# Gate and up by quads of eight products, three of the eight with seven, in a hybrid encoder layer

## The chip, the cores and the metric

The kernel runs on one core of one Trainium2 chip. The metric is device time in microseconds (us) of one execution; lower is better. Before the change it is 1369.25 us, the median of three runs (1369.16 to 1369.85).

The engines by their names in the profile: PE is TensorE (matmuls; PEld its loads of the stationary operand), DVE is VectorE, ACT is ScalarE, POOL is GpSimd, and SP issues most DMAs. PSUM is the memory that matmuls write, eight banks of 512 float32 values per partition; SBUF is the large on-chip memory.

## The reference

One encoder layer on 256 tokens of width 2048, float32. The part that the change is about is the second half, a SwiGLU feed-forward network of width 5632:

```python
gt, up = jnp.split(rms_norm(x, g_ffn) @ w_gate_up, 2, axis=-1)
return x + (jax.nn.silu(gt) * up) @ w_down
```

Ahead of it stand a combined input projection, two attentions of eight heads each (latent attention and dilated window attention), sigmoid gates, and an output projection `w_o` that is added to the residual stream.

## The kernel before, in words

**Products in three parts.** A float32 product is made of three float32r matmuls. Each operand is split into `h`, its rounded copy, and `l`, the remainder. `mm3` (L383 to L386) issues h x h, then `ah` with the other operand's `l`, then `al` with its `h`, all added up in one PSUM bank. A *block product* here is `mm3` of 128 tokens by 128 features with 128 features by up to 512 columns.

**Groups and chunks.** All projections are `Group`s: a weight, 512 columns of it, a range of 128-row blocks k, and a function that reads the result out (`evac`). Each group has a PSUM tile of two banks, one per half of the tokens (`psm`, two tiles, tag "main"); transposes and attention use `side` tiles of two banks (`pss`, two of them). A group is cut into chunks of `CK` = 2 blocks. Per chunk there are three steps:

- `load(i)` (L694 to L703): one DMA of 512 KB on SP's queue into a tile of 4 KB per partition.
- `split(i)` (L705 to L712): ACT casts the chunk to `wh` (L710), DVE subtracts to get `wl` (L711).
- `products(i)` (L718 to L743): 2 blocks x 2 halves of the tokens x 3 matmuls = 12 matmuls.

The pool `wp` holds `AHEAD + 1` = 4 buffers of each of `w`, `wh` and `wl`. The pool `tp` holds 34 tiles of 4 KB per partition for activations (`t4`).

**What sets the order.** Each engine runs its instructions in the order of the program (L90 turns scheduling off); only semaphores between engines hold it. The loop at L781 to L815 is that order: at step i it issues the load of chunk i + 4, the split of chunk i + 3, the products of chunk i, then the read-out if the chunk ends its group, then at most one piece of a waiting job (a transpose, a stage of an attention). A job is `ready` some steps after it was made; if a product needs it sooner, it is finished on the spot (L789). A tile's buffer is given to a new tile when the old one's last reader is done.

**The feed-forward part.** The 22 blocks of 512 columns of `w_gate_up` are 11 of gate and 11 of up (L668 to L674), each a group of 16 blocks: 8 chunks. `evac_gate` (L592) applies silu on ACT, `evac_up` (L600) multiplies on DVE, and a job transposes the result into `hidT` (`transpose_in`, L196), whose own split is L171 on ACT and L176 on DVE. The columns are done in two halves, of six and five blocks; after each half come four groups of `w_down`, added to the residual `x1` by `evac_down` (L615). `evac_wo` (L568) makes `x1`, and its job transposes it with the gain `g_ffn` into `hT`, split likewise.

## Time and profile before

| | before |
|---|---|
| median of 3 runs | 1369.25 us |
| span of the profiled execution | 1367.5 us |
| TensorE busy | 1356.5 us (99%), 6342 matmuls |
| DVE busy | 758.1 us (55%), 774 instructions |
| ACT busy | 623.5 us (46%), 776 instructions |
| POOL busy | 32.3 us (2%) |
| DMA | 257.14 MB, 188 GB/s, queue of SP busy 59.8% |

The span is the time from the first to the last instruction of one profiled execution. "L711 DVE ... wl<-w,wh 128x1024" means that line 711 of the kernel ran on DVE, read the tiles w and wh, wrote wl, with 128 partitions by 1024 elements; then come how often, the busy time in us, the mean duration in ns, and the idle time of the engine just before with what ended it. A line of a timeline has its start in us, its duration in us, the engine, the line and the operation. Matmuls overlap in the pipeline, so the distance between two starts is their price, and not the duration shown.

The feed-forward part begins at 634.4 us of the span, with the first product of `hT`, and reaches to its end.

### The profile page before, as it was taken

The numbers are of one execution on the slowest core, as the hardware profiler recorded it, in microseconds if no ns is written. First come the engines' busy times: TensorE is split into PE (matmuls) and PEld (weight loads), VectorE is DVE, ScalarE is ACT, GpSimd is POOL, SyncE is SP. The second block draws the span as 40 slices with busy tenths as digits, with TensorE's granted clock in tenths as the row PEclk, the third lists the DMA queues.
The fourth block names the chain that finished last, engine by engine and source line by source line (L and its number), as shares of the span: only waits on it lengthen the run. The fifth ranks groups of instructions, "written<-read, shape, count | busy, mean of one in ns | idle before, by whom it ended". The sixth has DMA issues, their size and how long they took to land.

```text
span 1367.5 us, 16361 instructions
## 1 busy us (share of the span) xinstructions
PE 1356.5 (99%) x6342; PEld 1144.7 (84%) x6342; DVE 758.1 (55%) x774; ACT 623.5 (46%) x776; POOL 32.3 (2%) x41
## 2 busy tenths in 40 slices
PE   7999999999999999999999999999999999999998
PEld 6899999888888888888888888888888888888887
DVE  5566777677655556555445544554444544555443
ACT  6555655454444444445444444433344444444332
POOL 1011111000000000000000000000000000000000
PEclk9999999999999999999999999999999999999999
DMA  8555555555566666565665665555665665565663
GB/s 259 175 173 168 158 172 177 174 166 172 178 202 199 198 190 216 193 210 181 196 192 182 191 198 184 187 189 193 194 193 187 194 197 188 186 188 183 202 212 123
DMA packets 138205, 257.14 MB, mean 188 GB/s; under 512 B 9192, under 2 KB 28688, under 8 KB 138128
## 3 DMA queue, kind: packets, MB, share of 16 engines
q1 hardware_dynamic: 137760, 255.96, 59.8%
q8 instruction: 49, 0.80, 0.2%
q14 instruction: 28, 0.23, 0.0%
q10 hardware_dynamic: 144, 0.13, 0.0%
q0 software_dynamic: 224, 0.01, 0.0%
HBM read 253.97 MB, written 2.10 MB: 187 GB/s over the span
## 4 chain that ended last, share of the span: by engine, by line
PE 99%; DMA 1%; SPq 0%; DVE 0%; issue 0%; ACT 0%; DVEq 0%
PE g L384 31%; PE g L386 31%; PE g L385 31%; PE tr_hid L201 1%; DMA w<-in_w_in_dram 1%; PE tr_hT L201 0%; PE tr_mT L201 0%; PE tr_xT L201 0%; DMA xn<-in_x_dram 0%; PE mla3s L386 0%; PE mla2s L386 0%; PE mla0s L386 0%; PE mla1s L386 0%; PE mla2s L385 0%; PE mla2s L384 0%; PE mla1s L385 0%
## 5 line engine op out<-in xcount | busy, mean ns | idle before, releaser
L711 DVE TENSOR_TENSOR wl<-w,wh 128x1024 fp32r<-128x1024 f32 (+2 forms) x481 | 575.6, 1201 | 472.8 <-ACT wh L710 470.8
L710 ACT CAST wh<-w 128x1024 fp32r<-128x1024 f32 (+2 forms) x481 | 496.2, 1036 | 537.6 <-PE g L386 489.7
L384 PE MATMUL g<-wh,hTh 128*128 128x512 f32 x704 | 274.8, 390 | 0.0
L386 PE MATMUL g<-wh,hTl 128*128 128x512 f32 x704 | 274.0, 389 | 0.0
L385 PE MATMUL g<-wl,hTh 128*128 128x512 f32 x704 | 273.9, 389 | 0.0
L384 PE MATMUL g<-wh,xTh 128*128 128x512 f32 (+1 forms) x544 | 210.2, 386 | 1.9 <-ACT xTh L173 1.9
L386 PE MATMUL g<-wh,xTl 128*128 128x512 f32 (+1 forms) x544 | 207.2, 381 | 0.5 <-DVE xTl L178 0.5
L385 PE MATMUL g<-wl,xTh 128*128 128x512 f32 (+1 forms) x544 | 207.2, 381 | 0.0
L386 PEld LDWEIGHTS g<-wh,hTl 128*128 128x128 f32 x704 | 132.1, 188 | 27.6
L385 PEld LDWEIGHTS g<-wl,hTh 128*128 128x128 f32 x704 | 132.2, 188 | 27.1
L384 PEld LDWEIGHTS g<-wh,hTh 128*128 128x128 f32 x704 | 132.2, 188 | 27.1
L384 PEld LDWEIGHTS g<-wh,xTh 128*128 128x128 f32 x544 | 102.7, 189 | 17.2 <-ACT xTh L173 2.1
L386 PEld LDWEIGHTS g<-wh,xTl 128*128 128x128 f32 x544 | 102.4, 188 | 17.3 <-DVE xTl L178 1.0
L385 PEld LDWEIGHTS g<-wl,xTh 128*128 128x128 f32 x544 | 102.6, 189 | 15.3 <-DVE wl L711 0.4
L384 PE MATMUL g<-wh,hid0h 128*128 128x512 f32 x192 | 74.8, 390 | 0.0
L386 PE MATMUL g<-wh,hid0l 128*128 128x512 f32 x192 | 74.7, 389 | 0.0
L385 PE MATMUL g<-wl,hid0h 128*128 128x512 f32 x192 | 74.7, 389 | 0.0
L384 PE MATMUL g<-wh,hid1h 128*128 128x512 f32 x160 | 62.3, 390 | 0.0
L386 PE MATMUL g<-wh,hid1l 128*128 128x512 f32 x160 | 62.2, 389 | 0.0
L385 PE MATMUL g<-wl,hid1h 128*128 128x512 f32 x160 | 62.2, 389 | 0.0
L384 PE MATMUL g<-wh,mTh 128*128 128x512 f32 x128 | 50.2, 392 | 0.0
L386 PE MATMUL g<-wh,mTl 128*128 128x512 f32 x128 | 49.8, 389 | 0.0
(509 smaller groups left out, 1233.5 us busy)
## 6 DMA issues: line engine op xcount, KB each, us to landing
w<-in_w_gate_up_dram SPq DMA_DIRECT2D x176, 512.0 KB, 4.5
w<-in_w_down_dram SPq DMA_DIRECT2D x88, 512.0 KB, 4.3
w<-in_w_in_dram SPq DMA_DIRECT2D x79, 512.0 KB, 4.2
w<-in_w_in_dram SPq DMA_DIRECT2D x56, 448.0 KB, 3.6
w<-in_w_o_dram SPq DMA_DIRECT2D x32, 512.0 KB, 4.5
w<-in_w_o_mla_dram SPq DMA_DIRECT2D x16, 512.0 KB, 4.1
w<-in_w_o_dil_dram SPq DMA_DIRECT2D x16, 512.0 KB, 4.2
w<-in_w_ukv_dram SPq DMA_DIRECT2D x8, 512.0 KB, 4.3
```

The lines of the kernel that those rows point to most:

```text
L201: nc.tensor.transpose(ps[:, k, t * P:(t + 1) * P], src(t, k0 + k), ident)
L384: nc.tensor.matmul(ps, ah, bh, start=first, stop=False)
L385: nc.tensor.matmul(ps, ah, bl, start=False, stop=False)
L386: nc.tensor.matmul(ps, al, bh, start=False, stop=last)
L710: nc.scalar.copy(h, t)
L711: nc.vector.tensor_sub(l, t, f32(h))
```

## The change: what it does

**Quads.** A group of gate and up now has 1024 columns: 512 of gate and the 512 of up that belong to them (a *pair*; there are 11). Its 16 blocks of rows are 8 pairs of blocks. One *quad* is two row blocks (k0, k1) by gate and up, with both halves of the tokens: eight block products. Five quads (0, 1, 2, 4, 6) are *plain* and make these eight, 24 matmuls. Three (3, 5, 7, `FAST`) are *fast*: seven block products of sums and differences of the operands, 21 matmuls. The seven products have a PSUM bank each, kept over the whole pair; plain quads add to four places, three of them shared with fast products (banks of products 3, 2 and 4) and one of their own (0). All eight banks are taken from the start of the feed-forward part to the end (`hold_banks`). Transposes then use banks that are idle at that time.

**What a fast quad needs.** `split_fast` splits three raw quarters of the chunk (512 + 1024 columns: two casts on ACT, two subtractions on DVE), then forms four sums in place (four DVE additions of 512 columns). Then `split` splits the four sums (2048 columns). `splits` issues `split_fast` of chunk c + 1 ahead of `split` of chunk c. On the side of the activations, `job_h` transposes `x1` by pairs of blocks; for fast quads it forms four differences of 128 columns and splits seven pieces.

**The end of a pair.** `evac_pair` combines the banks: a copy on ACT, eight DVE operations of 512 columns, silu on ACT, two multiplications on DVE. Bank 0 is copied by ACT after quad 6.

**Chunks.** `CK` is 4, so a chunk is 1 MB (8 KB per partition), loaded by two DMAs of 512 KB. There are three raw buffers (`xp`), six of split weights (`wp`: h and l of three chunks), and 28 tiles of 4 KB instead of 34. Splits are issued two chunks ahead (`AHEAD` = 2), loads up to four ahead. For jobs and their readiness a step is still two row blocks, or one quad.

**Parts.** The 11 pairs are done in five parts of 3, 2, 2, 2 and 2, each followed by its four groups of `w_down`. These go two at a time, their chunks alternating, except for the last two of all.

The core of the diff:

```diff
-CK = 2
-AHEAD = 3
+CK = 4
+AHEAD = 2
+PARTS = ((0, 3), (3, 5), (5, 7), (7, 9), (9, 11))
+NPAIR = KD // 2
+FAST = (3, 5, 7)
...
-    wp = ctx.enter_context(tc.tile_pool(name="wp", bufs=AHEAD + 1))
-    tp = ctx.enter_context(tc.tile_pool(name="tp", bufs=34))
+    tp = ctx.enter_context(tc.tile_pool(name="tp", bufs=28))
+    xp = ctx.enter_context(tc.tile_pool(name="xp", bufs=3))
+    wp = ctx.enter_context(tc.tile_pool(name="wp", bufs=6))
...
+    def hold_banks():
+        for n in "AB":
+            held[n] = psm.tile([P, NT, 512], F32, name=f"m{n}", tag="main")
+        for n in "CD":
+            held[n] = side(f"s{n}").rearrange("p (t n) -> p t n", t=NT)
+        held["q"] = {m: held[n][:, i] for n, ms in (("A", (1, 6)), ("B", (7, 5)), ("C", (3, 2)), ("D", (4, 0)))
+                     for i, m in enumerate(ms)}
...
+        if i not in FAST:
+            hP[i] = t4([P, 2, 2, S], f"hP{i}", F32R)
+            split_evac(*((hP[i][:, 0, k], hP[i][:, 1, k], ps[:, k], g[k]) for k in range(2)))
+        else:
...
+            nc.vector.tensor_sub(v[:, 3], v[:, 7], v[:, 2])
+            nc.vector.tensor_sub(v[:, 4], v[:, 7], v[:, 0])
+            nc.vector.tensor_sub(v[:, 5], v[:, 0], v[:, 3])
+            nc.vector.tensor_sub(v[:, 6], v[:, 1], v[:, 5])
+            split_pair(h, l, v[:, :7])
...
+    def evac_pair(half, i, last):
+        def evac(part, step):
+            q = held["q"]
+            z, u = t4([P, NT, 512], f"z{half}_{i}"), t4([P, NT, 512], f"u{half}_{i}")
+            add, sub = nc.vector.tensor_add, nc.vector.tensor_sub
+            nc.scalar.copy(u[:, 0], q[1])
+            sub(z[:, 0], q[6], u[:, 0])
+            add(u[:, 1], q[7], z[:, 0])
+            add(z[:, 0], q[5], z[:, 0])
+            add(z[:, 1], q[5], u[:, 1])
+            add(z[:, 0], q[3], z[:, 0])
+            add(z[:, 1], z[:, 1], part)
+            add(u[:, 0], q[2], u[:, 0])
+            sub(u[:, 1], q[4], u[:, 1])
...
+    def load(c):
+        g, gi, ks, q = chunks[c]
+        t = xt[c] = xp.tile([P, 4, 512], F32, name=f"x{c}", tag="x")
+        if q:
+            for kk in range(2):
+                src = g.w[(2 * q.i + kk) * P:(2 * q.i + kk + 1) * P].rearrange("p (n f) -> p n f", n=2)
+                nc.sync.dma_start(t[:, 2 * kk:2 * kk + 2], src[:, :, g.c0:g.c0 + 512])
+            return
...
+    def split_fast(c):
+        x = xt[c]
+        rh, rl, r = (t4([P, 2, 512], f"{n}{c}", F32R) for n in ("rh", "rl", "r"))
+        split_pair(rh, rl, x[:, 2:4])
+        split_pair(r[:, 0], r[:, 1], x[:, 1])
+        add = nc.vector.tensor_add
+        add(x[:, 1], x[:, 0], x[:, 1])
+        add(x[:, 0], x[:, 0], x[:, 2])
+        add(x[:, 2], x[:, 1], x[:, 2])
+        add(x[:, 3], x[:, 2], x[:, 3])
...
+    FACTOR = {1: 0, 2: 1, 4: 2, 5: 3, 7: 4, 6: 5, 3: 6}
+    PLAIN = {(0, 0): 3, (0, 1): 2, (1, 0): 0, (1, 1): 4}
...
+            for t, n in ((1, 0), (0, 0), (0, 1), (1, 1)):
+                m = PLAIN[t, n]
+                for kk in range(2):
+                    mm3(bank[m], hP[q.i][:, 0, kk, s], hP[q.i][:, 1, kk, s], h[:, 2 * kk + n], l[:, 2 * kk + n],
+                        q.first and kk == 0, q.last_plain and m == 0 and kk == 1)
...
+            for m in (1, 6, 7, 5, 3, 2, 4):
+                f = FACTOR[m]
+                mm3(bank[m], h[:, f], l[:, f], *w[m], q.first_fast and m in (1, 5, 6, 7), q.last)
...
+    def splits(to):
+        while ahead["split"] < min(to, n):
+            c = ahead["split"]
+            loads(c + 1)
+            if c + 1 < n and chunks[c + 1][3] and chunks[c + 1][3].fast and c + 1 not in raws:
+                loads(c + 2)
+                split_fast(c + 1)
+            split(c)
+            ahead["split"] += 1
...
+        if ks[0] == allks[0]:
+            loads(c + AHEAD + 2)
...
+        if ks[0] == allks[0]:
+            splits(c + AHEAD + 1)
+            loads(c + AHEAD + 3)
```

## The prediction

> **What bounds the kernel now.** I read the page's head and its chain first, then the waits of the engines and of the DMA queue.

> ```profile
> span 1367.5 us, 16361 instructions
> ...
> PE 1356.5 (99%) x6342; PEld 1144.7 (84%) x6342; DVE 758.1 (55%) x774; ACT 623.5 (46%) x776; POOL 32.3 (2%) x41
> ...
> PE 99%; DMA 1%; SPq 0%; DVE 0%; issue 0%; ACT 0%; DVEq 0%
> ```

> ```profile
> ACT wh L710 <- PE g L386: 489.7, 322, 4.4
> DVE wl L711 <- ACT wh L710: 470.8, 330, 7.0
> ```

> ```profile
> SPq L702 <- DVE wl L711: 1008.2, 442, 5.6
> ```

> The chain is TensorE from end to end, so every product removed there is time removed, as long as TensorE stays fed. The waits show how it is fed: ACT's cast (L710) waits for TensorE to free a buffer of split weights, DVE's subtraction (L711) waits for that cast, and the next weight load (L702) waits for that subtraction to free a raw buffer. It is a ring of load, cast, subtract, product, and today it has room: DVE is busy 55%. The span is 1367.5 us, the median 1369.25, so 1.75 us lie outside the span; I sum changes against the span and add 1.75.

> One chunk boundary in the timeline gives the pitch and the hand-overs:

> ```profile
> 950.58 0.39 PE L386 MATMUL g<-wh,hid0l 128*128 128x512 f32 x1
> ...
> 950.81 0.39 PE L384 MATMUL g<-wh,hid0h 128*128 128x512 f32 x1
> ...
> 951.01 1.05 ACT L710 CAST wh<-w 128x1024 fp32r<-128x1024 f32 x1 [1.67 <-PE g L386]
> ...
> 952.10 1.23 DVE L711 TENSOR_TENSOR wl<-w,wh 128x1024 fp32r<-128x1024 f32 x1 [1.49 <-ACT wh L710]
> ...
> 953.53 0.39 PE L384 MATMUL g<-wh,hid0h 128*128 128x512 f32 x1
> ```

> ```profile
> 639.87 1.03 PE L201 MATMUL tr_hT<-ident,x 128*128 128x128 f32 x8
> 640.66 0.47 PE L384 MATMUL g<-wh,hTh 128*128 128x512 f32 x1
> ```

> ```profile
> 546.39 1.22 DVE L711 TENSOR_TENSOR wl<-w,wh 128x1024 fp32r<-128x1024 f32 x1
> ...
> 547.63 1.78 SPq L702 DMA_DIRECT2D w<-in_w_o_dram  x2
> ```

> A chunk of 12 matmuls takes 953.53 - 950.81 = 2.72 us, 0.2267 us each (the 0.39 us are latencies that overlap). ACT starts 0.20 us after TensorE turns to the next chunk, DVE 0.04 us after ACT ends. Eight transposes cost 640.66 - 639.87 = 0.8 us. SP issues a load at once when DVE's subtraction ends (547.61 to 547.63); I allow 0.1.

> **What is removed.**

> ```profile
> L384 PE MATMUL g<-wh,hTh 128*128 128x512 f32 x704 | 274.8, 390 | 0.0
> ```

> L384, L385 and L386 run 704 times each for gate and up: 2112 matmuls, 192 per pair of column blocks, 11 pairs. After the change a pair has five plain quads of 24 and three fast ones of 21: 183. So 99 matmuls go: 99 x 0.2267 = **-22.4 us**. A pair's products then take 183 x 0.2267 = 41.48 us, a plain quad 5.44, a fast one 4.76. Transposes, weight bytes and down products stay the same in number.

> **What is added, and its prices.**

> ```profile
> L711 DVE TENSOR_TENSOR wl<-w,wh 128x1024 fp32r<-128x1024 f32 x415 | 506.6, 1224 | 457.0 <-ACT wh L710 455.7
> ...
> L604 DVE SCALAR_TENSOR_TENSOR sg<-g,r,sg 128x512 f32<-128x512 f32 x22 | 15.5, 747 | 4.6 <-PE g L386 4.6
> ...
> L176 DVE TENSOR_TENSOR hid0l<-tr_hid,hid0h 128x1024 fp32r<-128x1024 f32 x6 | 7.3, 1225 | 14.0 <-ACT hid0h L171 14.0
> ...
> L711 DVE TENSOR_TENSOR wl<-w,wh 128x512 fp32r<-128x512 f32 x2 | 1.4, 692 | 1.3 <-ACT wh L710 1.3
> ```

> ```profile
> L710 ACT CAST wh<-w 128x1024 fp32r<-128x1024 f32 x415 | 436.1, 1054 | 511.7 <-PE g L386 465.3 <-DMA w<-in_w_down_dram 28.9 <-DMA w<-in_w_in_dram 10.9
> ...
> L596 ACT ACTIVATE sg<-g,r 128x512 f32<-128x512 f32 x22 | 13.9, 686 | 16.7 <-PE g L386 16.7
> ...
> L710 ACT CAST wh<-w 128x512 fp32r<-128x512 f32 x2 | 1.2, 616 | 1.2 <-DMA w<-in_w_in_dram 1.2
> ```

> ```profile
> 644.13 2.35 DVE L711 TENSOR_TENSOR wl<-w,wh 128x1024 fp32r<-128x1024 f32 x2
> ```

> On DVE, 512 elements cost 0.69 us and 1024 cost 1.22, so a 2048-element split costs 1.22 + 2 x 0.53 = 2.29 (an estimate from these two rows); on ACT likewise 1.05 + 2 x 0.44 = 1.93. Reading PSUM (hid0l) costs the same as SBUF. Two DVE operations in a row take 2.35, not 2.45: the next one starts 0.09 early.

> Per pair DVE now has 8 splits (2.20 each), 3 fast extras (1.13 + 0.60 + four adds of 0.60 = 4.13), 8 operations of 0.60 and 2 of 0.66 at the end, and 1.13 for the transposed result: 17.6 + 12.4 + 6.1 + 1.1 = 37.2 us under 41.5 us of products. In sum DVE is not the bound. ACT has 8 x 1.93 + 3 x 1.67 + 4 of about 0.65 + 1.05 = 24 us. SP issues as many DMAs as before (two per 1 MB in place of one per 512 KB); POOL is not touched. What decides is order and buffers.

> **The order.** Raw chunks are now 1 MB in three buffers: the load of chunk n waits for the split S(n-3). Split weights have room for three chunks: S(n) waits for the end of quad n-3. And the fast extra F(n) is issued before S(n-1), so DVE's order in a pair is S0, S1, (end of the previous pair), F3, S2, S3, F5, S4, S5, F7, S6, S7. F5 needs load 5, which starts only when S2 is done, with only S3 in between; S4, which TensorE needs first, stands behind F5 on both engines. So the lookahead turns a load's latency into a wait. That latency:

> ```profile
> L702 SPq DMA_DIRECT2D w<-in_w_gate_up_dram x36: 367/368/368, 701.3 to 798.3; - x36
> ...
> DMA to landing us min/median/max: 3.3/4.5/4.9
> ```

> ```profile
> w<-in_w_gate_up_dram SPq DMA_DIRECT2D x176, 512.0 KB, 4.5
> ...
> xres<-in_x_dram SPq DMA_DIRECT2D x4, 512.0 KB, 6.3
> ```

> A quad's chunk is two 512 KB DMAs issued about 0.4 us apart. If the second lands as a lone one does: 4.5 + 0.4 = 4.9 us. If it fares like the residual, loaded beside a weight load: 6.3 + 0.4 = 6.7. I take the middle, **5.8 us**, and keep both ends.

> [...]

> **A first pair of a part**, with 0 at its first product. The last down result is added on DVE until 1.42. F3 runs 1.33 to 5.69 (chunk 3 has landed by then), S2 ends 7.89, before quad 2 at 10.88. Load 5: 7.99 to 13.79. F5: cast on ACT to 14.89, DVE 14.93 to 19.28; S4 ends 21.48 where quad 3 ended 21.08: wait 0.45. Load 7: 21.58 to 27.38; F7, then S6 to 35.08 where quad 5 ended 31.73: wait **3.40**. The pair takes 41.48 + 3.85 = 45.3.

> **A later pair** follows another pair. S1 ends at 0.20, because it stood behind the late S6 and its own load; then the eight end operations run back to back from 0.11. The fifth reads the bank that quad 0 wants as its second, at 1.36, and is done at 3.33: wait **2.02**. The two last multiplications end 6.45, F3 6.36 to 10.71, S2 12.91 (no wait: transposes lie there). Load 5 lands 18.81, F5 to 24.31, S4 to 26.51 where quad 3 ended 23.89: wait **2.67**. Load 7 lands 32.41, S6 at 40.10 where quad 5 ended 36.76: wait **3.39**. Sum of waits 8.1; with 0.8 of transposes, 50.4 us against 192 x 0.2267 + 0.8 = 44.3 before.

> **At a part's end** the down products want banks 1 and 6 at once; the operation that reads bank 6 starts late by the same delay: 0.9, and 0.2 for the transposes. The extra down additions (12 x 1.22 on DVE) lie under down chunks of 5.44 us that need 2.29 of DVE: nothing; uncovered, 15 us.

> Sum for gate, up and down: -22.4 + 18.5 (five first pairs, the very first 0.7 less) + 6 x 8.1 + 5 x 1.1 = **+50**.

> The three fast pieces of the normalised input cost DVE at most 3 x (4 x 0.60 + 1.22) = 11 us more, spread over the output projection and the first three quads, where a split's 2.29 us stands against 5.44 of products: nothing on the path, 11 if that cover were gone.

> **Elsewhere.** The start:

> ```profile
> 10.21 1.05 ACT L710 CAST wh<-w 128x1024 fp32r<-128x1024 f32 x1 [2.25 <-DMA w<-in_w_in_dram]
> ...
> 14.49 1.05 ACT L710 CAST wh<-w 128x1024 fp32r<-128x1024 f32 x1 [0.36 <-DMA w<-in_w_in_dram]
> ...
> 17.86 0.47 PE L384 MATMUL g<-wh,xTh 128*128 128x512 f32 x1
> ```

> Blocks 4 to 7 are now cast as one: not before 14.49, to 16.4 on ACT and 18.7 on DVE, where TensorE began block 4 at 17.86: +0.8, so +1. In attention a job's operation can stand behind a 2.29 us split instead of 1.22; the split is done 0.20 + 1.93 + 0.04 + 2.29 = 4.5 us after a chunk's start and jobs are read one step (2.72) or more later, so 0, at most 8 jobs x 1.1 = 9. Six fewer 4 KB tiles: the trace shows no such wait; 0, at most one step for each of 8 jobs, 22; DVE's 55% speaks for 0. Earlier loads could win back part of the 1% of DMA in the chain: at best -5.

> Span 1367.5 + 50 + 1 = 1418.5; with 1.75, **1420 us**.

> **Rivals.** *The loads stay hidden (faster).* Two quads take 10.2 us of products; from S(n-3) to S(n-1) the ring takes the landing time plus 1.1 + 4.3 + 2.3 = 7.7. At a landing of 2.5 us or less nothing waits at quads 4 and 6; only the end of pairs is left, 6 x 2.0 + 5 x 1.1 = 17.5, and the time is 1369.25 - 22.4 + 17.5 + 1 = 1365; without those too, 1348. For it: DVE's sum is under TensorE's. Against it: the shortest landing of even half a chunk is 3.3. Chance 0.14. *A wash*: with a landing near 3.2 us the waits are worth the 22 us: 1369, 0.06. *The waits cool TensorE's clock.*

> ```profile
> 5.30 0.77 PE L384 MATMUL g<-wh,xTh 128*128 128x512 f32 x1
> ...
> 6.97 0.63 PE L384 MATMUL g<-wh,xTh 128*128 128x512 f32 x1
> 7.40 0.63 PE L385 MATMUL g<-wl,xTh 128*128 128x512 f32 x1
> ...
> 10.15 0.39 PE L385 MATMUL g<-wl,xTh 128*128 128x512 f32 x1
> 10.38 0.40 PE L386 MATMUL g<-wh,xTl 128*128 128x512 f32 x1
> ...
> 13.81 0.50 PE L384 MATMUL g<-wh,xTh 128*128 128x512 f32 x1 [1.91 <-ACT xTh L173]
> ...
> 15.43 0.39 PE L384 MATMUL g<-wh,xTh 128*128 128x512 f32 x1
> 15.66 0.40 PE L385 MATMUL g<-wl,xTh 128*128 128x512 f32 x1
> ```

> At the start matmuls came every 0.43 us, half rate; after 1.91 us idle the full 0.23 was soon back. If each of the 11 waits of 3.4 us brought back half rate for about 5 us, as from the first product at 5.3 to 10.2, that is 11 x 2.5 = 27 us more: 1447, chance 0.08. [...]

> **How the numbers follow.** The forecast has 0.72. Its own ends: at 4.9 us of landing the same steps give +29 (1399), at 6.7 +78 (1449). The range reaches down to 1380, where the short landing (1399) meets pairs that end without the 17.5 us of waits above, and up to 1460, the long landing (1449) with attention's 9, which also holds the cooled clock; the faster case and the wash, 0.20, are left out. A difference of about 0.2% (2.7 us) can be told from none. Slower 0.72 + 0.08 = 0.80, same 0.06, faster 0.14.

> **What would show it.** Gate and up have 2013 matmuls. TensorE has idle time before the first product of quads 4 and 6, released by DVE's split, and at a pair's second bank, released by the end operations; ACT's cast in F waits for the gate and up DMA, SP for the split. If those waits are absent, or released by products only, the order argument is wrong; if the DMA lands in under 3 us, its size is.

## The result and the profile after

The changed kernel takes 1450.82 us (median of 4 runs, 1447.73 to 1452.78) against 1369.2 us: 1.059 times as long (95% interval 1.0575 to 1.0605). The forecast was 1420 in a range of 1380 to 1460, so sign and range held, and 31 us are missing. The profiled run, the fastest of the four, took 1447.73. Its page begins as follows; the last line is the chain of work that ended last, by engine:

```profile
span 1446.0 us, 15759 instructions
...
PE 1368.2 (95%) x6243; PEld 1140.3 (79%) x6243; DVE 945.1 (65%) x842; ACT 642.9 (44%) x628; POOL 31.4 (2%) x41
...
PE 72%; DVE 13%; DMA 6%; ACT 4%; issue 4%; SPq 1%; POOL 0%; DVEq 0%; ACTq 0%
```

The 99 matmuls are gone (6342 to 6243), yet TensorE is busier than before (1356.5): some matmuls ran slower (0.42 to 0.43 us from start to start at a granted clock of 0.50, 0.23 at 1.00). The chain was TensorE to 99%; now DVE, DMA and ACT hold 23% of it. The two largest waits of TensorE, and the one of ACT for loads (us in total, times, longest):

```profile
PE sD L424 <- DVE u L669: 31.0, 6, 5.2
PE sD L425 <- DVE wl L218: 24.9, 14, 3.1
...
ACT rh L217 <- DMA x<-in_w_gate_up_dram: 93.3, 20, 5.8
```

L669 is the last of the eight end operations that read a pair's banks, and the six waits are the six pairs that follow another in their part. The second row is quads 4 and 6 waiting for their split; the third is the cause the prediction named, ACT's cast in the fast quad's extra work (F) waiting for a load.

I add up the feed-forward from the starts of the matmuls: what a distance between two starts has beyond 0.2267 us counts as a wait, or as clock loss where matmuls run on at half the granted clock. The feed-forward took 733.1 us before and takes 805.9 now: -22.4 for the products, +73.9 of waits, +20.7 of clock loss, which makes 72.2 of the 72.8. It also starts later, at 640.1 in place of 634.4.

One boundary between two pairs, in time:

```profile
684.75 1.91 ACT L217 CAST wh<-x 128x2048 fp32r<-128x2048 f32 x1
...
686.70 2.29 DVE L218 TENSOR_TENSOR wl<-x,wh 128x2048 fp32r<-128x2048 f32 x1 [3.85 <-ACT wh L217]
...
688.61 0.39 PE L426 MATMUL sD<-wh,hsl 128*128 128x512 f32 x1
688.91 0.68 DVE L662 TENSOR_TENSOR z<-mA,u 128x512 f32<-128x512 f32 x1
...
693.42 0.68 DVE L669 TENSOR_TENSOR u<-sD,u 128x512 f32<-128x512 f32 x1
...
694.16 0.80 PE L424 MATMUL sD<-wh,hP 128*128 128x512 f32 x1 [5.16 <-DVE u L669]
...
695.18 0.63 PE L426 MATMUL sD<-wh,hP 128*128 128x512 f32 x1
695.60 0.63 PE L424 MATMUL sD<-wh,hP 128*128 128x512 f32 x1
```

DVE does the subtraction of the next pair's second split (686.70) before the first end operation (688.91). TensorE's first product goes to bank 0, yet it waits for L669, which reads bank 4: the two share the tile sD. Then matmuls come every 0.42 us, half rate (the granted clock is 0.50 from 694.1 to 697.5).

### The profile page after: what moved, and what is told of

It reads as the page before. It is cut to its first block, busy times and chain, and to the rows that moved or that the text cites. A ratio compares the mean times of both kernels' runs of the same rounds, so it can differ in the third digit from the quotient of the medians.

```text
span 1446.0 us, 15759 instructions
## 1 busy us (share of the span) xinstructions
PE 1368.2 (95%) x6243; PEld 1140.3 (79%) x6243; DVE 945.1 (65%) x842; ACT 642.9 (44%) x628; POOL 31.4 (2%) x41
## 4 chain that ended last, share of the span: by engine, by line
PE 72%; DVE 13%; DMA 6%; ACT 4%; issue 4%; SPq 1%; POOL 0%; DVEq 0%; ACTq 0%
PE g L426 12%; PE g L424 12%; PE g L425 12%; DVE wl L218 6%; DMA x<-in_w_gate_up_dram 5%; PE sC L424 4%; PE sC L425 4%; PE sC L426 4%; PE mA L424 3%; PE mA L426 3%; PE mA L425 3%; PE sD L425 2%; PE sD L426 2%; PE sD L424 2%; ACT wh L217 2%
## 5 line engine op out<-in xcount | busy, mean ns | idle before, releaser
L218 DVE TENSOR_TENSOR wl<-x,wh 128x2048 fp32r<-128x2048 f32 (+3 forms) x242 | 537.3, 2232 | 272.9 <-ACT wh L217 269.0
L217 ACT CAST wh<-x 128x2048 fp32r<-128x2048 f32 (+3 forms) x242 | 450.2, 1864 | 338.8 <-PE g L425 107.9
L424 PE MATMUL sD<-wh,hP 128*128 128x512 f32 x220 | 90.4, 411 | 31.0 <-DVE u L669 31.0
L426 PEld LDWEIGHTS g<-wh,xTl 128*128 128x128 f32 x544 | 102.5, 188 | 18.2 <-DVE xTl L214 2.2
L425 PEld LDWEIGHTS g<-wl,xTh 128*128 128x128 f32 x544 | 102.6, 189 | 17.6 <-DVE wl L218 2.7
L425 PE MATMUL sD<-wl,hP 128*128 128x512 f32 x220 | 90.9, 413 | 24.9 <-DVE wl L218 24.9
L424 PE MATMUL sC<-wh,hP 128*128 128x512 f32 x220 | 91.4, 415 | 0.0
L426 PE MATMUL sD<-wh,hP 128*128 128x512 f32 x220 | 89.9, 409 | 0.0
L425 PE MATMUL sC<-wl,hP 128*128 128x512 f32 x220 | 89.9, 408 | 0.0
L426 PE MATMUL sC<-wh,hP 128*128 128x512 f32 x220 | 88.8, 404 | 0.0
L424 PEld LDWEIGHTS sD<-wh,hP 128*128 128x128 f32 x220 | 42.9, 195 | 42.1 <-DVE u L669 33.5
L217 ACT CAST rh<-x 128x1024 fp32r<-128x1024 f32 x33 | 34.5, 1047 | 93.3 <-DMA x<-in_w_gate_up_dram 93.3
L425 PEld LDWEIGHTS sD<-wl,hP 128*128 128x128 f32 x220 | 43.3, 197 | 38.9 <-DVE wl L218 30.8
L425 PEld LDWEIGHTS sC<-wl,hP 128*128 128x128 f32 x220 | 44.8, 204 | 10.1
L424 PEld LDWEIGHTS sC<-wh,hP 128*128 128x128 f32 x220 | 44.5, 202 | 10.1
L426 PEld LDWEIGHTS sC<-wh,hP 128*128 128x128 f32 x220 | 44.0, 200 | 10.0
L426 PEld LDWEIGHTS sD<-wh,hP 128*128 128x128 f32 x220 | 43.5, 198 | 8.9
## 6 DMA issues: line engine op xcount, KB each, us to landing
x<-in_w_gate_up_dram SPq DMA_DIRECT2D x176, 512.0 KB, 4.8
x<-in_w_down_dram SPq DMA_DIRECT2D x88, 512.0 KB, 5.0
x<-in_w_in_dram SPq DMA_DIRECT2D x79, 512.0 KB, 4.7
x<-in_w_o_dram SPq DMA_DIRECT2D x32, 512.0 KB, 4.8
x<-in_w_o_mla_dram SPq DMA_DIRECT2D x16, 512.0 KB, 4.6
x<-in_w_o_dil_dram SPq DMA_DIRECT2D x16, 512.0 KB, 4.7
x<-in_w_ukv_dram SPq DMA_DIRECT2D x8, 512.0 KB, 4.5
```

The lines of the kernel that those rows point to most:

```text
L217: nc.scalar.copy(h, x)
L218: nc.vector.tensor_sub(l, x, f32(h))
L424: nc.tensor.matmul(ps, ah, bh, start=first, stop=False)
L425: nc.tensor.matmul(ps, ah, bl, start=False, stop=False)
L426: nc.tensor.matmul(ps, al, bh, start=False, stop=last)
```

## The experiments

**Theory.** Three mechanisms of order, and one that follows from them: F stands ahead of the previous quad's split and waits for a young load (waits at quads 4 and 6); the end operations stand behind a split, and bank 0 is held with bank 4 (boundaries); waits of 2 us or more halve the clock (in the changed kernel's feed-forward 13 of the 17 waits of 1.96 us or more had half rate behind them). **Rivals:** DVE has too much to do; 1 MB loads are too slow in any order; the half-rate spells have nothing to do with the waits.

Times with an interval are medians of four executions. The others are of a single execution, where the four of the changed kernel lie within 5.05 us.

**Lookahead off.** F is issued right before its own quad's split.

```diff
             loads(c + 1)
-            if c + 1 < n and chunks[c + 1][3] and chunks[c + 1][3].fast and c + 1 not in raws:
-                loads(c + 2)
-                split_fast(c + 1)
             split(c)
```

> The extra work for a fast quad (F) is issued right before that quad's own split, no longer before the split of the quad ahead of it. Order theory: the waits at the first product of quad 6 (2.1 to 3.3 us each, 25.6 in sum) and at quad 4 go, because no split stands behind a load that has just been issued; the six waits of 5.32 us between two pairs of a part stay, since they come from DVE working on the next pair's splits before the end operations. TensorE's work and waits in the feed-forward then fall by about 27 us, and with them about half of the 20.7 us that half-rate spells cost: about 1409 us, range 1398 to 1422. Rival 'DVE has too much to do': the amount of work is the same, so the time stays near 1450. Rival 'loads of 1 MB land too late in any order': quads 4 and 6 keep waits of 2 us or more, time over 1435.

Measured 1407.64 us, as expected. The wait at the boundary is all that is left of the two large ones:

```profile
PE sD L424 <- DVE u L669: 31.2, 6, 5.4
```

No wait at quads 4 and 6 is left (in the very first pair quads 3, 5 and 7 wait 0.84 to 1.35); the boundaries stay at 5.32 or 5.33 (5.53 once), waits fall to 44.6 and clock loss to 10.0. That is what the theory of order had; either rival would have left the time above 1435.

**End operations first.** In the main loop, for a pair's last quad:

```diff
-        if ks[0] == allks[0]:
+        late = q and q.last
+        if ks[0] == allks[0] and not late:
             splits(c + AHEAD + 1)
...
             g.evac(ps, i)
+            if late:
+                splits(c + AHEAD + 1)
+                loads(c + AHEAD + 3)
```

> At the last quad of a pair the end operations are issued before the splits and loads of that step, no longer after them; the lookahead stays. Order theory: the first product of the next pair waits about 1.9 us in place of 5.32 (six times: 20 us less), but the waits at quads 4 and 6 remain, and at quad 4 of a later pair some 1.4 us come back since the split chain starts later: waits in sum about 56 in place of 74 us, and half-rate spells after the six boundaries go (about 10 of the 20.7 us): about 1421, range 1410 to 1435. Rival 'bank ordering at the boundary is caused by TensorE's products themselves, not by DVE's order': boundary waits stay at 5.3 and the time near 1450.

Measured 1441.66: a miss, since the gain was to be 29 us and is 9. TensorE's waits:

```profile
PE sD L425 <- DVE wl L218: 37.2, 20, 4.1
PE sD L424 <- DVE u L669: 15.1, 6, 2.5
```

The boundaries halved (31.0 to 15.1), but quads 4 and 6 took most of it back (24.9 to 37.2). I read this so: while the lookahead stands, the ring of load, F and split sets the pace, and a wait saved ahead of it comes back at it.

**Both orders.** The two edits together.

> Both edits of order at once; the tile shapes, the number of products, of DVE and ACT operations, of bytes and of buffers are those of the changed kernel. Order theory: only six boundary waits of about 1.9 us and five of 0.8 at part ends are left, 16 us in place of 74, and without waits of 2 us or more the half-rate spells go too: 1358 to 1368 us, that is slightly faster than the kernel before (1369.2). Rival 'DVE has too much to do' or 'the loads land too late': over 1400. Rival 'the half-rate spells do not depend on the waits': about 20 us of clock loss remains, 1380 or more.

Measured 1384.73: a miss, between the theory (1358 to 1368) and the first two rivals (over 1400). The two edits give 66 us, more than 43 and 9 apart. The waits at quads 4 and 6 of later pairs stay away, but the six at the boundary are 2.68 to 3.33 where 1.9 was expected:

```profile
PE sD L424 <- DVE u L669: 16.0, 6, 3.2
```

Each is followed by a spell at half rate (behind the first, matmuls come 0.43 us apart). The time alone would also fit the third rival (1380 or more), but the clock loss is 8.7 us, not the 20 that it had.

**The boundary filled.** The changed kernel with matmuls whose result is overwritten:

```diff
             h, l = w
+            if q.first and chunks[c - 1][3]:
+                for m in range(16):
+                    nc.tensor.matmul(bank[(1, 6)[m % 2]], lhsT=hP[0][:, 0, 0, :P], rhs=h[:, 0], start=True, stop=True)
```

> The changed kernel with 16 added matmuls of 128 by 512 (3.6 us at 0.2267 each, into two banks that are free by then and whose values are overwritten, so nothing of the result depends on them) at the start of each pair that follows another pair of its part, six times. They fit inside the wait of 5.32 us. Theory that waits cause the half-rate spells: the boundary wait keeps its end, so the work is no later, but the spells that follow the six boundaries (from 694.1, 745.3, 912.6, 1055.9, 1202.7 and 1346.0 us, 30.7 us at half rate) go: 8 to 14 us faster, about 1438. Rival 'the spells come from something else than idle time, such as the amount of work': as many spells as before and about 1450, or more by the added matmuls. If the wait were set by TensorE itself and not by DVE, the time would rise by 6 x 3.6 = 22 us.

Measured 1444.09. The windows of two former spells, in the changed kernel and then in this one (columns: length, busy time of PE, PEld, DVE, ACT and POOL, granted clock, DMA share, GB/s):

```profile
694.10:697.50 3.40, 3.34 (x8) 2.67 (x9) 2.94 (x5) 3.40 (x5) 0.00 (x0) 0.50 0.00 0
...
745.30:752.10 6.80, 4.52 (x11) 3.56 (x12) 6.70 (x11) 4.59 (x5) 0.00 (x0) 0.50 0.27 104
```

```profile
694.10:697.50 3.40, 2.81 (x13) 1.98 (x12) 2.93 (x5) 3.39 (x6) 0.00 (x0) 1.00 0.18 68
745.30:752.10 6.80, 6.21 (x28) 4.81 (x27) 6.76 (x11) 4.61 (x5) 0.00 (x0) 1.00 0.42 149
```

All six spells behind boundaries are gone, with the same work behind them (a granted clock of 1.00 where it was 0.50): idle time makes them. Clock loss fell from 20.7 to 10.6. The time is 3.6 below the profiled 1447.73, where 8 to 14 had been expected, and 3.6 is within the spread of the changed kernel's own times. The waits at quads 4 and 6 grew from 24.9 to 30.4: a faster TensorE arrives earlier at the same ring.

**Banks exchanged, both orders.** Two things change beside the order: the banks that share a tile are now 1+6, 7+0, 3+2 and 4+5, and the end operations follow the order in which products finish.

```diff
-("B", (7, 5)), ("C", (3, 2)), ("D", (4, 0))
+("B", (7, 0)), ("C", (3, 2)), ("D", (4, 5))
-        spare.extend((1, 6, 7, 5))
+        spare.extend((1, 6))
+            add(z[:, 0], q[3], z[:, 0])
+            add(u[:, 0], q[2], u[:, 0])
             add(z[:, 0], q[5], z[:, 0])
             add(z[:, 1], q[5], u[:, 1])
-            add(z[:, 0], q[3], z[:, 0])
             add(z[:, 1], z[:, 1], part)
-            add(u[:, 0], q[2], u[:, 0])
```

> Both edits of order, and banks 0 and 5 change places (the pairs that share a tile are now 1+6, 7+0, 3+2, 4+5), with the end operations in the order in which the fast products finish. Theory that a hold acts on a pair of banks that share a tile: the first product of the next pair (bank 0) now waits only for the second end operation (in the run with both orders that ended 0.4 us before TensorE needed it), so the six waits of 2.68 to 3.33 us go, and with them the six half-rate spells that followed each (8.5 us lost): 1384.7 - 16 - 8.5 - about 3 = 1357, range 1352 to 1364, faster than the kernel before. Rival 'the products wait bank by bank, and bank 4 is simply late' or 'DVE is short of time at the boundary': waits of 2 us or more remain at the second to fourth bank, 1370 or more. Rival 'spells come with the load on TensorE, not with waits': spells remain, 1365 or more.

Measured 1389.58, 1.0145 times the kernel before (1.0128 to 1.0162): a clear miss (1352 to 1364 was expected), and no faster than without the banks. The waits for end operations are indeed gone, and others stand in their place:

```profile
PE mB L425 <- DVE wl L218: 16.4, 11, 1.8
PE mA L425 <- DVE wl L218: 3.9, 5, 1.2
```

TensorE now waits for splits, at the boundary and at part ends. DVE in the middle of a pair shows why:

```profile
700.99 0.69 DVE L836 TENSOR_TENSOR x<-x 128x512 f32<-128x512 f32 x1
703.73 2.29 DVE L218 TENSOR_TENSOR wl<-x,wh 128x2048 fp32r<-128x2048 f32 x1 [2.05 <-ACT wh L217]
```

After the fourth addition of F (L836), ACT casts the whole chunk (1.9 us) while DVE stands idle for 2.05; so it is at all three fast quads. In the 46 us from 695 to 741 DVE is busy 38.52, and with the three gaps that makes 44.7. This points to a hand-over from DVE to ACT and back as the bound, rather than to DVE's work or the loads. The lookahead had covered it: in the changed kernel the quad ahead has its subtraction right behind L836 (at 700.63), and the fast quad's own split follows with a gap of 0.36.

**Lookahead off and banks exchanged**, the end operations left behind the split:

> Lookahead off and banks 0 and 5 exchanged, but the splits are still issued before the end operations. Tile theory: the end operations still start late, about 0.4 us after the last product, but bank 0 waits only for the second of them: about 1.7 us in place of 5.33 at each of six boundaries, the other banks wait no longer, and spells after waits this short are rarer or gone: 1407.6 - 22 - 5 to 10 = 1371 to 1381, likeliest 1376. If bank 0 was held by bank 0's own use and not by bank 4's, nothing changes: 1407.

Measured 1386.81, 21 us less than with lookahead off alone, of which 10 are clock loss:

```profile
PE mB L424 <- DVE u L663: 6.4, 6, 1.6
PE mA L425 <- DVE wl L218: 6.0, 8, 1.2
```

The first product of a pair still goes to bank 0, but it now waits for L663, which reads bank 7, the new neighbour in its tile. These waits are 0.95 (1.79 and 1.80 in the first part) in place of 5.33, and no spell at half rate is left in the feed-forward. So what holds a product back acts on both banks of a tile together. The first two end operations are the same in the old and the new order, so this shorter wait comes from the pairing; what the new order of the others adds to the 21 us was not run apart. The time is 6 us beyond the range. Waits of 0.85 to 0.95 at quads 3 and 7 of later pairs (1.56 once) are new and make 11 us; they stand behind splits that the hand-over delays.

**The plain feed-forward.** Chunks, parts, tiles and start of the change, with gate and up computed as before.

```diff
-    gi = 0
-    while gi < len(groups):
...
+    for gi, g in enumerate(groups):
+        for ks in chunk_ks(g):
+            add_chunk(gi, ks)
```

> One part of the change alone: 8 KB chunks, five parts, 28 tiles and the new start, but gate and up computed as in the kernel before (eight products per block, two banks per column block, 2112 matmuls). Order theory: the loss lies in the quads, so this kernel is close to the one before: its 1370.9 on this chip plus the 5.65 us that the changed kernel loses ahead of the feed-forward, plus 0 to 4 for three more part ends: 1378, range 1372 to 1386. Rival 'the 1 MB loads through three buffers are too slow for TensorE wherever they are used': more than 1395, with TensorE waiting for DVE's split in the feed-forward. Rival 'the loss ahead of the feed-forward comes from the quads' own pieces': 1372 or less.

Measured 1387.01, 1 us above the range. No product of the feed-forward waits for a split, so the 1 MB loads are not slow as such. The loss of 6 us ahead of the feed-forward is here too, so the quads do not cause it. The other 12 us are waits of about 8.6, nearly all at four part ends, and 3.0 of clock loss behind the last two of these. Down columns one after another reach the last block's transposed result too early (TensorE waits 1.1 us for ACT's cast of it and 0.5 for DVE's subtraction). The changed kernel runs two columns side by side and has no such wait for the cast, so I put this share down to the arrangement of this run; that was not tested.

**The old start**, beside the run with both orders and the banks:

```diff
-    g_in(0, 512, evac_lat("cq"), sizes=[1, 1, 2, 4, 4, 4])
+    g_in(0, 512, evac_lat("cq"), sizes=[1, 1, 2, 2, 2, 2, 2, 2, 2])
```

> The kernel with both orders and the exchanged banks, and the first column block of the input projection loaded in the sizes of the kernel before (1, 1, then 2 blocks each, in place of 1, 1, 2, 4, 4, 4). If the changed sizes cost the 2.4 us of the start (TensorE waits until 18.59 us for blocks 4 to 7 that are cast as one), the feed-forward starts 2 to 2.5 us earlier and the time is that much shorter, about 1354. If the start is bound by the bytes that have to land (three buffers now hold half as much), it is unchanged or up to 3 us longer.

Measured 1384.82 (1.0109 times the kernel before, 1.0094 to 1.0124), 4.8 less, and so a miss of the 1354 that had been worked out from the expected time of the run beside it. The edit itself does more than expected: the feed-forward starts at 636.1 in place of 640.4, so the start had cost more than the 2.4 I had read off.

**Raw chunks in two tiles.** On the run with lookahead off and banks exchanged (1386.81), with six tiles of 4 KB in place of three of 8 KB:

```diff
-        t = xt[c] = xp.tile([P, 4, 512], F32, name=f"x{c}", tag="x")
+        t = xt[c] = [xp.tile([P, 2, 512], F32, name=f"x{c}_{o}", tag="x") for o in range(0, 4 if q else len(ks), 2)]
...
-        split_pair(h[s], l[s], t[s])
+        for o in range(0, nk, 2):
+            m = min(2, nk - o)
+            split_pair(h[:, o:o + m, :w], l[:, o:o + m, :w], t[o // 2][:, :m, :w])
```

> The kernel without lookahead and with exchanged banks, and a raw chunk now held in two tiles of 4 KB in place of one of 8 KB (six of them, same memory), cast and subtracted in two pieces. Hand-over theory, formed after the last four runs: without the lookahead DVE stands idle 2.05 us before each fast quad's split, because ACT casts the whole chunk only after DVE's fourth addition, and DVE's 38.5 us of work per pair plus three such gaps fill the pair's 46 us, so that a wait taken away in one place comes back at the next. With two tiles ACT casts the first half while DVE does the third and fourth addition; the gap before the split falls to 0.3 us or less, TensorE's waits of 0.85 to 0.95 us at quads 3 and 7 and at the pair's start go for the most part: 1386.8 - 15 = 1372, range 1362 to 1379. Rival 'DVE's busy time is the bound': two subtractions of 1.22 in place of one of 2.29 add some 8 to 10 us of DVE in all, no wait shrinks, 1387 to 1395. Rival 'it is the loads': TensorE's waits remain with ACT's casts waiting for the DMA, 1380 or more.

Measured 1352.27 us, 20 better than expected, outside the range on the fast side, and faster than the kernel before. DVE at the same place:

```profile
701.78 0.69 DVE L836 TENSOR_TENSOR x<-x 128x512 f32<-128x512 f32 x1
702.39 4.70 DVE L218 TENSOR_TENSOR wl<-x,wh 128x1024 fp32r<-128x1024 f32 x4
```

There is no gap; four subtractions run on at once. In the same 45.5 us DVE is busier than with the 8 KB tiles (first row: the run with these; second: this one), with TensorE busy throughout:

```profile
688.00:733.50 45.50, 43.27 (x191) 34.80 (x191) 37.59 (x36) 23.65 (x20) 0.00 (x0) 1.00 0.50 171
```

```profile
688.00:733.50 45.50, 45.50 (x206) 37.34 (x205) 42.74 (x50) 24.20 (x28) 0.00 (x0) 1.00 0.64 207
```

The feed-forward falls from 744.8 to 714.8 us, and its waits from about 34 to 5. The other 4.5 of the 34.5 us lie ahead of it: it starts at 635.7 in place of 640.3. The rival that DVE's busy time is the bound falls: DVE is busy 959.7 us in the whole run where it was 946.0, and the run is faster. The halves may also be freed and loaded sooner, but that is not what was lacking: even with the 8 KB tiles no cast of the feed-forward is shown waiting for a load.

**All edits**, with two end operations ahead of the last quad's splits, and the old start:

> As the run with half tiles, and two end operations (those that read banks 1, 6 and 7) issued before the last quad's splits, the other six behind them; the start has the chunk sizes of the kernel before. Hand-over theory: the next pair's first bank is free before TensorE wants it, and the next quad's split is no later than in the run without the edit, so boundary waits of 0.95 us and part ends of about 1 us fall under 0.3; with the start some 4 us earlier (the feed-forward began at 636.1 in place of 640.4 with these sizes) the time is 1372 - 12 - 3 = 1357, range 1350 to 1366: faster than the kernel before by about 12 us. Rival 'DVE's busy time is the bound': 1375 or more, with waits of 2 us at the second quad of each pair as in the run with both orders and exchanged banks.

Measured 1358.75, 0.9917 of the kernel before (0.9899 to 0.9935). That lies in the range by luck: 1357 was 15 us less than the 1372 expected for the last run, which took 1352.27, and against that the edits cost 6.5. The mechanism was a miss. At the boundary:

```profile
717.66 0.69 DVE L662 TENSOR_TENSOR z<-mA,u 128x512 f32<-128x512 f32 x1 [3.13 <-ACT u L661]
718.45 0.69 DVE L663 TENSOR_TENSOR u<-mB,z 128x512 f32<-128x512 f32 x1
719.06 2.35 DVE L218 TENSOR_TENSOR wl<-x,wh 128x1024 fp32r<-128x1024 f32 x2
721.33 0.68 DVE L665 TENSOR_TENSOR z<-sC,z 128x512 f32<-128x512 f32 x1
```

DVE, ahead of TensorE by now, stands 3.13 us before an operation whose products are not done, and the split that it could have done stands behind it, as that split's cast does on ACT behind the copy of bank 1 (copy at 717.04, cast at 717.52). The other end operations come later for it, and bank 3 waits 1.06 at every boundary.

**Without that edit**, the old start kept:

> The run with half tiles at 1352.3 (TensorE waits only 4.9 us in its feed-forward) with one more edit: the chunk sizes of the start as in the kernel before. With these sizes the feed-forward began at 633.0 in the last run, against 635.7 without: 2.7 us earlier, and nothing behind it changes, so 1349.6, range 1347 to 1352. If the last run's later end (1358.8) came from these sizes and not from the two end operations put first, it is 1356 or more.

Measured 1349.65 us, 0.9854 of the kernel before (0.9837 to 0.9872): the fastest version here, and where it was expected. So the two end operations put first cost about 9 us. Its chain is TensorE again:

```profile
PE 1336.8 (99%) x6243; PEld 1125.2 (84%) x6243; DVE 959.6 (71%) x1081; ACT 667.8 (50%) x867; POOL 32.8 (2%) x41
...
PE 98%; DMA 0%; ACT 0%; DVE 0%; SPq 0%; issue 0%; DVEq 0%
```

**Half tiles alone**, all orders and banks as in the change:

> The changed kernel with nothing but the raw chunk in two tiles of 4 KB: lookahead, banks and the order of the end operations as in the change. Order theory: the fast quad's extra work still stands before the split of the quad ahead, so the wait for its load stays, shortened by at most the 1.1 us by which the first half is freed earlier; the boundary waits stay at 5.3; time 1432, range 1412 to 1446. Rival 'the 8 KB tile is the whole cause': the hand-over from DVE to ACT is what costs in every order, and the time falls below 1390 by this edit alone.

Measured 1418.08, in the range of the theory of order (1412 to 1446) and far from the 1390 of the rival. The waits of both kinds are there still, smaller (the rows that in the changed kernel have 31.0 and 24.9), and ACT's wait for loads in F is no smaller (96.9 where it was 93.3):

```profile
PE sD L424 <- DVE u L669: 26.2, 6, 4.4
PE sD L425 <- DVE wl L218: 14.8, 20, 2.0
```

So the tile's size is not the whole cause; order and banks count too. Which of these two the half tiles still need was not run.

A fourth raw buffer, with the lookahead kept, was not tried either, so how much of the waits at quads 4 and 6 comes from having three stays open.

## Why the prediction came out as it did

- **Products removed, 22.4 us.** Right: 99 fewer. Of the 19.65 us by which the fastest version beats the kernel before, 18.2 are in the feed-forward (733.0 to 714.8); the others come ahead of it.
- **"What decides is order and buffers", not DVE's sum.** Right, and shown: the same products, with more DVE work, take 1349.65 or 1450.82 by order, banks, tiles and the sizes of the start alone.
- **First pairs of a part.** Right to half a microsecond from the second part on: 0.34 to 0.46 at quad 4 and 2.95 to 3.29 at quad 6, where 0.45 and 3.40 were worked out with a landing of 5.8. In the second part ACT's cast in F starts 5.3 us (quad 5) and 5.6 us (quad 7) after the first of the two loads was issued, so the landing was sized well. One load's own median rose from 4.5 to 4.8 us. The very first pair waited 3.37 at quad 3 in their place, for the fast pieces of the normalised input that the prediction had put at nothing.
- **Later pairs.** The sum was right by luck (8.1 predicted; 5.32, 0.37 right behind it, and 2.1 to 2.3 at quad 6 measured), and its steps were wrong. The step "the bank that quad 0 wants as its second, at 1.36 [...] wait 2.02" failed: the end operations did run back to back from the last product as worked out, but the first product waits for the eighth of them, because banks 0 and 4 are one tile. The 3.3 us more at the boundary then gave the splits time, so quad 4 waited nothing in place of 2.67, and quad 6 2.1 to 2.3 in place of 3.39. The errors cancelled.
- **At a part's end.** Right: 0.81 measured at each of five, 0.9 worked out.
- **Elsewhere, +1.** Mis-sized: 5.65. The start explains 4.3 of it by the run that has its old sizes beside both orders, 3.0 by the one beside the half tiles; the rest was not taken apart.
- **The clock.** This was a rival at 0.08, and it came true together with the forecast: 20.7 us, where the rival had 27. The forecast itself put nothing on the clock, an estimate that no run had shown; in the changed kernel 13 of 17 waits of 1.96 us or more had half rate behind them, for 3.413 or 6.827 us each. With 73.9 of waits for the predicted 72.6, the clock (20.7) and the start (4.65 too little) are nearly the whole of the 27.7 us that the sum lacked for the profiled run; the median lies 3.1 above that run.
- **Loads hidden, and the wash.** Wrong for the change as it stands. Once order, banks, tiles and the start were changed, the time was 1349.65, close to the 1348 that this rival had given for no waits at all. Part of that is chance: some 4 us of waits are left, and the start gained 1.7 where 1 more had been reckoned.

## What to carry to other kernels

When waits are removed one at a time, ask which chain sets the pace: a saving ahead of it comes back at it, as at the filled boundary and with the end operations first. An operation issued early is only early if its inputs are there; until then it holds up everything behind it on its engine (the lookahead's F behind a load, ACT's cast up to 5.8 us; the two end operations behind products, DVE 3.13). In these runs the unit that was waited for is the tile: two banks in one tile were released together (bank 0 waited 5.33 us with bank 4 in its tile, mostly 0.95 with bank 7), and two halves of a chunk in one tile too (DVE idle 2.05 us before the fast quad's split, with two tiles none). Pairing the banks otherwise, with the end operations reordered, was worth 21 us here, and splitting the chunk 34.5, 30 of them in the feed-forward.

## What the hardware showed

```profile
728.06 0.39 PE L424 MATMUL sD<-wh,hP 128*128 128x512 f32 x1
730.53 0.50 PE L425 MATMUL sD<-wl,hP 128*128 128x512 f32 x1 [2.08 <-DVE wl L218]
...
732.33 0.63 PE L425 MATMUL sC<-wl,hP 128*128 128x512 f32 x1
732.76 0.63 PE L426 MATMUL sC<-wh,hP 128*128 128x512 f32 x1
```

```profile
782.02 0.39 PE L424 MATMUL sD<-wh,hP 128*128 128x512 f32 x1
784.46 0.51 PE L425 MATMUL sD<-wl,hP 128*128 128x512 f32 x1 [2.05 <-DVE wl L218]
...
785.74 0.39 PE L424 MATMUL sC<-wh,hP 128*128 128x512 f32 x1
785.97 0.39 PE L425 MATMUL sC<-wl,hP 128*128 128x512 f32 x1
```

The first lies inside the stretch between edges that ends at 731.7; this has 2.37 us of idle time, and half rate follows. The second is cut by an edge at 782.9; the stretch behind it has 1.77, and nothing follows. Over the feed-forward of the changed kernel (13 falls to half rate, without the one at the end of the run), counted from the starts of the matmuls, a full-rate stretch with 2.26 us of idle time or more was always followed by half rate, one with 1.87 or less never; none lay between the two.
